# Computing the first norm in two token halves, with the token matrix loaded by halves around the first weights

## The chip, the cores and the metric

The kernel runs on one core of a Trainium2 chip. A core has five engines that each work through their own list of instructions in order: TensorE (PE in the profile, its weight loads PEld), VectorE (DVE), ScalarE (ACT), GpSimd (POOL) and SyncE (SP, which here does nothing but issue DMA transfers). Engines wait for each other through semaphores. The metric is the time of one execution on the device in microseconds (us); the median of three runs before the change is 925.3 us (924.67 to 925.98).

## The reference

One transformer layer for 128 context tokens and 512 latent tokens with 1024 features. The part that matters here is its beginning:

```python
def _rmsnorm(x, g):
    xf = x.astype(jnp.float32)
    inv = lax.rsqrt(jnp.mean(xf * xf, axis=-1, keepdims=True) + RMS_EPS)
    return (xf * inv).astype(x.dtype) * g
...
    sh1, sc1, g1, sh2, sc2, g2 = _modulation(c, w_mod, b_mod)   # silu(c) @ w_mod + b_mod
    h = _rmsnorm(x, n1) * (1 + sc1) + sh1
    aq, ak, av, bq, bk, bv, ga, gb = _mixer_inputs(h, w_in, qg, kg)   # h @ w_in, split
```

Context tokens and latent tokens have their own modulation vectors (`c_ctx` and `c`). Attention of two kinds, a merge, a second norm and an MLP follow; the change does not touch them.

## The kernel before

**Layout.** Features lie on the 128 partitions, tokens along the row: the token matrix is eight feature tiles of 128 x 640 (`NT = 640` columns, 128 context tokens and then 512 latent ones). `HALVES` are columns 0 to 319 and 320 to 639, which is as many as one matmul here writes (128x320). `SEGS[h]` cuts a half further where the two groups of tokens meet: half 0 is 128 + 192 columns, half 1 is 320, and `SEGS[2]` is the whole row as 128 + 512.

**Precision.** Operands of the large products are split in two, a high part (rounded to TensorE's short type, fp32r) and a low part (what is left). A product is three matmuls: high weights with high h, low weights with high h, high weights with low h.

**The stage in question** is the first 51 us. `squares` builds the mean of squares: ScalarE squares one feature tile, VectorE the next, VectorE adds them, and a matmul with a matrix of 1/1024 (`ones`, in full float32) sums over the partitions into `mean[h]`, once per half. `rstd_rows(h)` turns that into the reciprocal root with two ScalarE instructions (logarithm, exponential). For each feature tile f, `mod_product(f, q)` multiplies the conditioning vector with a 512 KB block of modulation weights (four matmuls for each of two blocks q), `mod_rows` copies the result out of PSUM, `mod_cols` (two matmuls) turns rows into columns, and two small VectorE instructions make scale and shift. `h_scaled` (VectorE) multiplies x by scale and reciprocal root into `xm`, `h_hi` (ScalarE) adds the shift and rounds (h0h, h1h, ... in the profile), `h_lo` (VectorE) makes the low part (h0l, ...).

`first_gemm(f, i, part)` multiplies feature tile f with three tiles of the input projection (i = 0, 1, 2) while the later modulations are computed; `w0_conv(q)` splits their weights for two feature tiles at a time, the high part on ScalarE, the low part on VectorE. One feature tile is 18 matmuls: for each of three weight tiles and each of two halves, three products. `warm(n)` issues n matmuls of `ones` by `ones` whose result nobody reads, from the table `WARM`; they are called fillers below.

**Order.** All this stands under `tc.manual_schedule`: each engine executes its instructions in the order in which the code writes them. SyncE issues loads in the order of the calls `x_load`, `mod_load`, `w0_load`; each transfer reuses one of eight semaphores, so a transfer is issued only when the one eight places ahead has landed.

Of the kernel before, what the change touches and what calls it, by code (L numbers as in the profile page):

```python
# [10 lines left out]
F32 = mybir.dt.float32  # L11
F32R = mybir.dt.float32r
AF = mybir.ActivationFunctionType
# [3 lines left out]
P = 128  # L17
NT = 640
HT = 320
KT = 8  # L20
# [25 lines left out]
OU = 1800  # L46
MG = 2
W2P = 2
WARM = (15, 3, 2, 5, 0, 0, 3)
NMS = 9  # L50
W0P = 0
WAH = (4, 6)
# [17 lines left out]
HALVES = (slice(0, HT), slice(HT, NT))  # L70
# [3 lines left out]
def trunk_layer(ctx: ExitStack, tc: tile.TileContext, xT, small_in, wmodA, wmodB, tabs, cacheK, cacheV, bias,  # L74
                w_in, w_br, w_out, w1, w2, yT, akT, avT, bkT, bvT):
    nc = tc.nc
    PE, ACT, DVE = nc.tensor, nc.scalar, nc.vector
# [29 lines left out]
    def u(name, dt=F32):  # L107
        return cur["p"].tile([P, NT], dt, tag="u", bufs=cur["nu"], name=name)
# [39 lines left out]
    p0 = open_phase("p0", 9)  # L148
# [8 lines left out]
    ones = cst.tile([P, P], F32, name="ones")  # L157
# [8 lines left out]
    def mod_load(f, qs=range(2)):  # L166
        for q in qs:
            st = p0.tile([P, 1024], F32, tag="ms", bufs=NMS, name="ms")
            nc.sync.dma_start(st, wmodA[f, :, q * 1024:(q + 1) * 1024])
            MS[f, q] = st  # L170

    def w0_load(q):
        for n in FIRST:
            W0S[n, q] = p0.tile([P, 256], F32, tag="ws", bufs=6, name="ws")
            nc.sync.dma_start(W0S[n, q], w_in[n][:, q * 256:(q + 1) * 256])

    xs = []

    def x_load(i):
        x = p0.tile([P, 2, NT], F32, tag="x2", bufs=4, name=f"x{i}")  # L180
        nc.sync.dma_start(x, xT[:, 2 * i:2 * i + 2, :])
        xs.extend(x[:, j] for j in range(2))
# [168 lines left out]
    b0 = [f() for f in (ps_s, ps_s, ps_s, ps_t, ps_g, ps_g)]  # L351
    acc0 = [(b0[2 * i][:, :HT], b0[2 * i + 1][:, :HT]) for i in range(3)]
    H1, rows, ss, xm, rstd = [], {}, {}, {}, u("rstd")

    def warm(n):

        for _ in range(n):
            PE.matmul(acc0[2][1][:, :P], ones, ones, start=True, stop=True)

    def mod_product(f, q):  # L360

        for k in range(4):
            g = 32 * k
            PE.matmul(pm[f % 2][g:g + 2, :256], sc_e[:, 4 * q + k], MS[f, q][:, k * 256:(k + 1) * 256],
                      start=q == 0, stop=q == 1, tile_position=(0, g))

    def mod_rows(f, eng=ACT):
        rows[f] = p0.tile([P, 256], F32, tag="mrow", bufs=2, name="mrow")
        if eng is DVE:
            for sl in (slice(P, 2 * P), slice(0, P)):  # L370
                DVE.tensor_copy(rows[f][:, sl], pm[f % 2][:, sl])
        else:
            ACT.activation(rows[f], pm[f % 2][:, :256], AF.Copy)

    def mod_cols(f):
        p = pm[f % 2]
        for i in (1, 0):
            PE.matmul(p[:, 256 + 2 * i:258 + 2 * i], rows[f][:, i * P:(i + 1) * P], sel, start=True, stop=True)
# [5 lines left out]
    SEG0 = SEGS[0] + SEGS[1]  # L384

    def h_scaled(f):
        xm[f] = u("xm")
        for sl, g in SEGS[2] if f else SEG0:
            DVE.scalar_tensor_tensor(xm[f][:, sl], xs[f][:, sl], ss[f][1][:, g:g + 1], rstd[:, sl],
                                     op0=OP.mult, op1=OP.mult)  # L390

    def h_hi(f, segs=None):
        if len(H1) == f:
            H1.append(h_pair(f"h{f}"))
        for sl, g in segs or SEGS[2]:
            ACT.activation(H1[f][0][:, sl], xm[f][:, sl], AF.Identity, bias=ss[f][0][:, g:g + 1])

    def h_lo(f):
        for sl, g in SEGS[2]:
            DVE.scalar_tensor_tensor(H1[f][1][:, sl], xm[f][:, sl], ss[f][0][:, g:g + 1], r32(H1[f][0][:, sl]),  # L400
                                     op0=OP.add, op1=OP.subtract)

    def first_gemm(f, i, part, hs=(0, 1)):

        ws = W0[i] if part == 0 else W0[i][:1]
        for w, h in [(w, h) for h in hs for w in ws] if f == 0 else [(w, h) for w in ws for h in hs]:
            PE.matmul(acc0[i][h], w[:, f], H1[f][part][:, HALVES[h]], start=f == 0 and w is W0[i][0] and part == 0,
                      stop=f == KT - 1 and part == 1)

    def w0_conv(q, tiles=range(3), parts="hl"):  # L410
        for i in tiles:
            ks = slice(2 * q, 2 * q + 2)
            st = W0S[FIRST[i], q].rearrange("p (k n) -> p k n", k=2)
            if "h" in parts:
                ACT.activation(W0[i][0][:, ks], st, AF.Copy)
            if "l" in parts:
                (DVE, nc.gpsimd)[W0P].tensor_sub(W0[i][1][:, ks], st, r32(W0[i][0][:, ks]))

    def squares(i, between=None):

        q, q2 = u("sq"), u("sq")
        ACT.activation(q, xs[2 * i], AF.Square)
        DVE.tensor_mul(q2, xs[2 * i + 1], xs[2 * i + 1])
        for sl in HALVES if i == 3 else (slice(0, NT),):
            DVE.tensor_add(q[:, sl], q[:, sl], q2[:, sl])
        for h in range(2):
            PE.matmul(mean[h][:, :HT], ones, q[:, HALVES[h]], start=i == 0, stop=i == 3)
            if between and h == 0:
                between()
# [14 lines left out]
    with tc.manual_schedule(engines={e.engine for e in (PE, ACT, DVE, nc.gpsimd, nc.sync)}):  # L444
        for f in range(2, KT):
            mod_load(f)
            if f % 2 == 0:
                w0_load(f // 2)
        for p in pm:
            DVE.memset(p[:, :256], 0.0)  # L450
        ACT.activation(sc_e, cc, AF.Exp, scale=-1.0)
        DVE.tensor_scalar(sc_e, sc_e, 1.0, None, op0=OP.add)
        DVE.reciprocal(sc_e, sc_e)
        DVE.tensor_mul(sc_e, sc_e, cc)
        DVE.tensor_scalar(b1, bm, 1.0, None, op0=OP.add)
# [11 lines left out]
        warm(WARM[4])  # L467
        mod_cols(0)
        warm(WARM[5])
        h_scaled(0)  # L470
        h_hi(0, SEG0)
        mod_product(1, 0)
        warm(WARM[6])
        w0_conv(0, (2,), "h")
        w0_conv(0, (1, 2), "l")
        first_gemm(0, 0, 0, (0,))
        mod_product(1, 1)
        first_gemm(0, 0, 0, (1,))
        mod_rows(1)
        h_lo(0)  # L480
        first_gemm(0, 1, 0)
        mod_cols(1)
        h_scaled(1)
        first_gemm(0, 2, 0)
        h_hi(1)
        for i in range(3):
            first_gemm(0, i, 1)
        for q in range(2):
            mod_product(2, q)
        mod_rows(2)  # L490
        h_lo(1)
        w0_conv(1)
        for f in range(1, KT - 1):
            if f + 2 < KT:
                first_gemm(f, 0, 0)
            mod_cols(f + 1)
            h_scaled(f + 1)
            if f + 2 < KT:
                mod_product(f + 2, 0)
            else:  # L500
                first_gemm(f, 0, 0)
            first_gemm(f, 1, 0)
            if f + 2 < KT:
                mod_product(f + 2, 1)
            h_hi(f + 1)
            if f + 2 < KT:
                mod_rows(f + 2)
            first_gemm(f, 2, 0)
            for i in range(3):
                first_gemm(f, i, 1)  # L510
            h_lo(f + 1)
            if f % 2 == 0 and f < KT - 2:
# [644 lines left out]
    for n in range(KT):  # L1157
# [17 lines left out]
        for h in range(2):  # L1175
            sl = HALVES[h]
# [613 lines left out]
```

## Time and profile before

| | us |
|---|---|
| median of three runs | 925.3 |
| the profiled execution | 923.14 |
| its span in the profile | 921.4 |
| PE busy in the span | 903.8 (98%) |
| opening fillers on PE | 1.06 to 6.58 |
| first square sum on PE | 7.86 |
| first matmul with h (feature tile 0) | 18.34 |
| first matmul of feature tile 1 | 23.33 |
| first matmul of feature tile 2 | 27.89 |
| first matmul with the next weights (L315) | 51.53 |

The profile is of one execution. Lines are L numbers of the kernel; a row names engine, line, operation, output, inputs and shape. A full float32 matmul is recorded as two instructions, so that 30 recorded fillers are 15 in the program. After the change the same code has other line numbers: the matmuls of fillers, squares, modulation, columns and feature tiles are L358, L427, L364, L378 and L407 before, and L356, L426, L362, L376 and L405 after.

### The profile page before, as it was taken

Reading aid. Unit: us, or ns where it says so; the run is one execution under the profiler, and the core shown is the slowest. Engines: PE = TensorE matmul, PEld = TensorE weight load, DVE = VectorE, ACT = ScalarE, POOL = GpSimd, SP = SyncE. Lnnn points to the kernel's source line nnn. Section 1 sums busy time; section 2 is a strip of 40 time slices with the busy share of each in tenths; the row PEclk is TensorE's granted clock in tenths of the full one; section 3 lists DMA queues with packets and bytes.
Section 4 is the critical chain, followed back from the end, with each engine's and each line's share of the span. In section 5 each row is a group of like instructions: output and inputs, shape, how many; then the busy total and the mean of one; then the engine's idle time right before and its main releaser. Section 6 shows DMA issues by size and latency. Waiting matters only on the chain.

```text
span 921.4 us, 16641 instructions
## 1 busy us (share of the span) xinstructions
PE 903.8 (98%) x6136; PEld 872.6 (95%) x6136; DVE 712.9 (77%) x1503; ACT 564.4 (61%) x1175; POOL 194.6 (21%) x225
## 2 busy tenths in 40 slices
PE   8999999999999999999999999999999999999996
PEld 6799889989999999999999999999999999999995
DVE  6675887857766697586689996986798778975897
ACT  4566777757656765755324577536754576447775
POOL 0020200002211001211130010445234432364140
PEclk9999999999999999999999999999999999999998
DMA  9893310115636389899742362888678877888475
GB/s 344 307 247 97 89 46 26 62 57 153 163 109 149 115 242 308 208 248 261 247 144 92 104 194 92 138 193 190 168 138 188 179 173 158 167 179 189 96 123 152
DMA packets 54321, 150.56 MB, mean 163 GB/s; under 512 B 6688, under 2 KB 10416, under 8 KB 54240
## 3 DMA queue, kind: packets, MB, share of 16 engines
q1 hardware_dynamic: 31440, 99.74, 32.9%
q0 software_dynamic: 21648, 48.45, 29.8%
q10 hardware_dynamic: 1152, 1.31, 0.4%
q8 instruction: 48, 0.79, 0.3%
q14 instruction: 33, 0.27, 0.1%
HBM read 137.15 MB, written 4.60 MB: 154 GB/s over the span
## 4 chain that ended last, share of the span: by engine, by line
PE 83%; DVE 7%; ACT 4%; DMA 3%; issue 2%; POOL 0%; DVEq 0%; SPq 0%; ACTq 0%; POOLq 0%
PE b L1657 12%; PE b L1658 12%; PE b L1659 12%; PE pg L315 6%; PE pg L316 6%; PE pg L317 6%; PE pss L317 3%; PE pss L315 3%; PE pss L316 3%; DVE mt L1102 2%; DMA wmt<-wmodB 2%; PE pt L317 2%; PE pt L315 2%; PE pt L316 2%; PE pt L694 1%
## 5 line engine op out<-in xcount | busy, mean ns | idle before, releaser
L1394 ACT ACTIVATE wb<-wsb 128x512 fp32r<-128x512 f32 x140 | 87.2, 628 | 89.5 <-PE b L1659 61.0
L1657 PE MATMUL b<-op,wb 128*128 128x320 f32 x448 | 138.6, 309 | 0.2 <-DVE x L1510 0.2
L1658 PE MATMUL b<-op,wb 128*128 128x320 f32 x448 | 138.5, 309 | 0.0
L1659 PE MATMUL b<-op,wb 128*128 128x320 f32 x448 | 138.4, 309 | 0.0
L1399 DVE TENSOR_TENSOR wb<-wsb,wb 128x512 fp32r<-128x512 f32 x124 | 91.5, 742 | 26.4 <-ACT wb L1394 26.3
L1402 POOL DMA_DIRECT2D wsb<-w x84 | 73.6, 911 | 128.6 <-DVE wb L1399 102.7
L1102 DVE SCALAR_TENSOR_TENSOR mt<-wmt,cb 128x512 f32<-128x512 f32 x128 | 80.7, 687 | 6.2 <-DMA wmt<-wmodB 6.2
L267 ACT ACTIVATE wh<-wst 128x512 fp32r<-128x512 f32 (+1 forms) x84 | 61.0, 740 | 39.7 <-PE pg L316 15.0
L1657 PEld LDWEIGHTS b<-op,wb 128*128 128x128 f32 x448 | 84.1, 188 | 0.9 <-DVE x L1510 0.9
L1658 PEld LDWEIGHTS b<-op,wb 128*128 128x128 f32 x448 | 84.1, 188 | 0.2 <-DVE op L1467 0.2
L1659 PEld LDWEIGHTS b<-op,wb 128*128 128x128 f32 x448 | 84.1, 188 | 0.0
L1379 POOL DMA_DIRECT2D wsb<-w x28 | 25.6, 914 | 137.2 <-DVE wb L1399 48.0
L633 DVE TENSOR_TENSOR pl<-pt,ph 128x512 fp32r<-128x512 f32 (+1 forms) x72 | 44.9, 627 | 12.0 <-ACT ph L632 10.1
L276 DVE TENSOR_TENSOR wl<-wst,wh 128x512 fp32r<-128x512 f32 (+1 forms) x55 | 43.0, 793 | 10.8 <-ACT wh L267 8.8
L1510 DVE SCALAR_TENSOR_TENSOR x<-b,parts,x 128x128 f32<-128x128 f32 (+1 forms) x116 | 46.3, 429 | 2.8 <-PE b L1659 2.0
L632 ACT ACTIVATE ph<-pt 128x512 fp32r<-128x512 f32 (+1 forms) x72 | 39.2, 548 | 13.9 <-PE po L702 3.9
L1394 ACT ACTIVATE wb<-wst 128x512 fp32r<-128x512 f32 x56 | 34.8, 626 | 16.2 <-PE b L1659 8.9
L1659 PE MATMUL b<-t,wb 128*128 128x320 f32 x144 | 44.5, 309 | 0.0
L1658 PE MATMUL b<-t,wb 128*128 128x320 f32 x144 | 44.5, 309 | 0.0
L1657 PE MATMUL b<-t,wb 128*128 128x320 f32 x144 | 44.5, 309 | 0.0
L1467 DVE TENSOR_TENSOR op<-hid,op 128x1280 fp32r<-128x1280 f32 (+2 forms) x32 | 36.9, 1155 | 7.6 <-ACT op L1466 7.4
L1510 DVE SCALAR_TENSOR_TENSOR x<-tp,parts,x 128x320 f32<-128x320 f32 (+2 forms) x60 | 38.5, 670 | 1.0 <-ACT tp L1561 1.0
(886 smaller groups left out, 3006.7 us busy)
## 6 DMA issues: line engine op xcount, KB each, us to landing
wsb<-w POOLq DMA_DIRECT2D x112, 256.0 KB, 5.2
wst<-w SPq DMA_DIRECT2D x36, 512.0 KB, 4.0
wmt<-wmodB SPq DMA_DIRECT2D x32, 512.0 KB, 4.4
wst<-w_in SPq DMA_DIRECT2D x31, 512.0 KB, 4.4
wsb<-w SPq DMA_DIRECT2D x28, 512.0 KB, 4.3
ms<-wmodA SPq DMA_DIRECT2D x16, 512.0 KB, 7.7
wl<-w_in POOLq DMA_DIRECT2D x9, 512.0 KB, 8.4
wst<-w_br SPq DMA_DIRECT2D x8, 512.0 KB, 6.5
```

The costliest lines, as they stand in the source:

```text
L267: ACT.activation(hi[:, ks], st[:, ks], AF.Copy)
L315: PE.matmul(ps, wh[:, k], xh[:, sl], start=first, stop=False)
L316: PE.matmul(ps, wh[:, k], xl[:, sl], start=False, stop=False)
L317: PE.matmul(ps, wl[:, k], xh[:, sl], start=False, stop=last)
L1102: DVE.scalar_tensor_tensor(t, st[:, q * 512:(q + 1) * 512], 1.0, r32(cb[2 * q + i][:, :512]), op0=OP.mult, op1=OP.mult, accum_out=parts[:, ...
L1394: ACT.activation(w[:, 0:4], t, AF.Copy)
L1399: (nc.gpsimd if o in BLKPOOL[l - 1] else DVE).tensor_sub(w[:, 4:8], t, r32(w[:, 0:4]))
L1402: nc.gpsimd.dma_start(t, self.src(l, c, n, e)[:, 4 * half:4 * half + 4], accum_op=OP.add)
L1510: DVE.scalar_tensor_tensor(X1[i][:, sl], src[:, sl.start - off:sl.stop - off], g[:, j:j + 1], X1[i][:, sl], op0=OP.mult, op1=OP.add)
L1657: PE.matmul(b, w[:, k], xh, start=not whole and k == 0, stop=False, skip_group_check=True)
L1658: PE.matmul(b, w[:, k], xl, start=False, stop=False, skip_group_check=True)
L1659: PE.matmul(b, w[:, 4 + k], xh, start=False, stop=o not in ("A11", "S2", "S1") and k == 3, skip_group_check=True)
```

## The change

The token matrix is loaded by halves: four transfers for the first 320 columns of all tiles, then the two modulation blocks of tile 0 and the first weights, then four transfers for the other columns. `squares(i, h)` works on one half at a time. The order of the work is written anew: the first half goes through squares, reciprocal root, scaling and rounding; its high part is multiplied with the high weights of feature tile 0 while the second half is squared; the second half follows. For the last two pairs of tiles in the second half VectorE does not add the two squares, and PE sums both (`whole` false). `WARM` changes, and two accumulators change places in PSUM (`b0`). The loop over feature tiles is written anew too.

```diff
-WARM = (15, 3, 2, 5, 0, 0, 3)
+WARM = (15, 2, 4, 3, 13, 2, 2)
...
-    for i in range(3):
-        x_load(i)
-    mod_load(0, (0,))
-    x_load(3)
-    mod_load(0, (1,))
+    def x_load(h):
+        for i in range(4):
+            nc.sync.dma_start(x2[i][:, :, HALVES[h]], xT[:, 2 * i:2 * i + 2, HALVES[h]])
+
+    x_load(0)
+    mod_load(0)
     w0_load(0)
+    x_load(1)
     mod_load(1)
...
+    def squares(i, h, whole=True):
+
+        t = u("sq")
+        q, sl = [t[:, x] for x in HALVES], HALVES[h]
+        ACT.activation(q[0], xs[2 * i][:, sl], AF.Square)
+        DVE.tensor_mul(q[1], xs[2 * i + 1][:, sl], xs[2 * i + 1][:, sl])
+        if whole:
+            DVE.tensor_add(q[0], q[0], q[1])
+        for j in range(1 if whole else 2):
+            PE.matmul(mean[h][:, :HT], ones, q[j], start=i == 0, stop=i == 3 and (whole or j == 1))
...
         warm(WARM[0])
-        for i in range(3):
-            squares(i)
-            warm(WARM[i + 1])
+        for i in range(4):
+            squares(i, 0)
+            warm(WARM[1])
         mod_product(0, 0)
-        squares(3, lambda: mod_product(0, 1))
-        w0_conv(0, (0,))
+        warm(WARM[2])
+        mod_product(0, 1)
         rstd_rows(0)
         mod_rows(0, DVE)
+        w0_conv(0, (0,), "h")
+        warm(WARM[3])
+        mod_cols(0)
+        h_scaled(0, 0)
         w0_conv(0, (1,), "h")
+        warm(WARM[4])
+        h_hi(0, 0)
+        w0_conv(0, (2,), "h")
+        for i in range(3):
+            first_gemm(0, i, 0, (0,), "h")
+        for i in range(4):
+            squares(i, 1, i < 2)
+            warm(WARM[5])
+        w0_conv(0, parts="l")
         rstd_rows(1)
...
+        for i in range(3):
+            first_gemm(0, i, 0, (0,), "l")
+        h_lo(0, 0)
         mod_product(1, 0)
+        mod_product(1, 1)
+        mod_rows(1)
+        h_scaled(0, 1)
+        h_hi(0, 1)
+        for i in range(3):
+            first_gemm(0, i, 1, (0,))
         warm(WARM[6])
         first_gemm(0, 0, 0, (1,))
...
         for f in range(1, KT - 1):
-            if f + 2 < KT:
-                first_gemm(f, 0, 0)
-            mod_cols(f + 1)
...
+            first_gemm(f, 0, 0)
+            if f == 1:
+                mod_product(2, 0)
+                mod_product(2, 1)
+                mod_rows(2)
+                w0_conv(1, parts="h")
             else:
+                mod_cols(f + 1)
+                h_scaled(f + 1)
...
             for i in range(3):
                 first_gemm(f, i, 1)
+            if f < 3:
+                for q in range(2):
+                    mod_product(f + 2, q)
+                mod_rows(f + 2)
             h_lo(f + 1)
+            if f == 1:
+                w0_conv(1, parts="l")
```

How this moves PE's list. In the rows, `ones` with 128x128 is a filler, `sq` a square sum, `ms` a modulation block, `mrow` the columns step, `w_...` the split weights (even numbers high, odd numbers low), and x15 says how often a row stands in succession. PE before the first matmul with h, from behind the opening fillers, before:

```order
L427 MATMUL pss<-sq,ones 128x320 x2
L358 MATMUL pg<-ones 128x128 x5
L364 MATMUL po<-ms,sc_e 2x256 x4
L427 MATMUL pss<-sq,ones 128x320
L364 MATMUL po<-ms,sc_e 2x256 x4
L427 MATMUL pss<-sq,ones 128x320
L378 MATMUL po<-pk,mrow 128x2 x2
L364 MATMUL pt<-ms,sc_e 2x256 x4
L358 MATMUL pg<-ones 128x128 x3
L407 MATMUL pss<-h0h,w_114 128x320
```

and now:

```order
L362 MATMUL po<-ms,sc_e 2x256 x4
L356 MATMUL pg<-ones 128x128 x4
L362 MATMUL po<-ms,sc_e 2x256 x4
L356 MATMUL pg<-ones 128x128 x3
L376 MATMUL po<-pk,mrow 128x2 x2
L356 MATMUL pg<-ones 128x128 x13
L405 MATMUL pss<-h0h,w_118 128x320
L405 MATMUL pt<-h0h,w_120 128x320
L405 MATMUL pg<-h0h,w_122 128x320
```

Ahead of the first h there were 15 + 13 fillers and 8 square sums; now there are 15 + 28 fillers and 4 square sums. The rows that follow on PE now, where feature tile 0 had its 18 matmuls in a piece with the modulation blocks of tile 1 between them:

```order
L426 MATMUL pss<-sq,ones 128x320
L356 MATMUL pg<-ones 128x128 x2
L426 MATMUL pss<-sq,ones 128x320
L356 MATMUL pg<-ones 128x128 x2
L426 MATMUL pss<-sq,ones 128x320 x2
L356 MATMUL pg<-ones 128x128 x2
L426 MATMUL pss<-sq,ones 128x320 x2
L356 MATMUL pg<-ones 128x128 x2
L405 MATMUL pss<-h0h,w_119 128x320
L405 MATMUL pt<-h0h,w_121 128x320
L405 MATMUL pg<-h0h,w_123 128x320
L362 MATMUL pt<-ms,sc_e 2x256 x8
```

Six square sums and eight fillers stand between the first three matmuls of tile 0 and the next three; two more fillers come further down. On VectorE, at the same place in the program, now:

```order
L386 SCALAR_TENSOR_TENSOR xm<-x_82,sc_249,rstd 128x320
L378 TENSOR_SCALAR sc_337<-pt,b_112,pk 128x2
L379 TENSOR_SCALAR sh_336<-pt,pk 128x2
L386 SCALAR_TENSOR_TENSOR xm<-x_82,sc_337,rstd 128x128
L386 SCALAR_TENSOR_TENSOR xm<-x_82,sc_337,rstd 128x512
L397 SCALAR_TENSOR_TENSOR h0l<-xm,sh_248,h0h 128x320
```

The low part of tile 0 in its second half (last row) stands behind the scale, the shift and the scaling of tile 1; before, the low part of tile 0 stood ahead of them.

More of the change, by code (lines that the diff above doesn't have):

```diff
@@ L175, in w0_load @@
             nc.sync.dma_start(W0S[n, q], w_in[n][:, q * 256:(q + 1) * 256])
[L177 to L182, printed above, removed]
-    for i in range(3):
-        x_load(i)
-    mod_load(0, (0,))
-    x_load(3)
-    mod_load(0, (1,))
+    x2 = [p0.tile([P, 2, NT], F32, tag="x2", bufs=4, name=f"x{i}") for i in range(4)]
+    xs = [x[:, j] for x in x2 for j in range(2)]
+    def x_load(h):
[3 more added lines that the diff above has]
+    mod_load(0)
     w0_load(0)
+    x_load(1)
     mod_load(1)
@@ L417, in w0_conv @@
                 (DVE, nc.gpsimd)[W0P].tensor_sub(W0[i][1][:, ks], st, r32(W0[i][0][:, ks]))
[L419 to L429, printed above, removed]
+    def squares(i, h, whole=True):
[7 more added lines that the diff above has]
+            PE.matmul(mean[h][:, :HT], ones, q[j], start=i == 0, stop=i == 3 and (whole or j == 1))
     def rstd_rows(h):
```

70 lines of the change are left out of this document (30 added, 40 removed).

## The prediction

> **What bounds the kernel now.** I read the page first, then the engines' busy time by stretches of the first 50 us, what PE waited for there, and the chain of waits through them.
>
> ```profile
> span 921.4 us, 16641 instructions
> PE 903.8 (98%) x6136; PEld 872.6 (95%) x6136; DVE 712.9 (77%) x1503; ACT 564.4 (61%) x1175; POOL 194.6 (21%) x225
> ...
> 6.60:18.30 11.70, 10.24 (x70) 6.83 (x70) 8.42 (x18) 5.84 (x13) 0.00 (x0) 1.00 1.01 374
> 18.30:27.90 9.60, 9.56 (x85) 7.00 (x86) 7.18 (x19) 5.07 (x12) 0.00 (x0) 1.00 1.04 397
> 27.90:50.00 22.10, 22.10 (x185) 17.71 (x184) 14.08 (x38) 12.29 (x28) 1.55 (x2) 1.00 0.75 255
> ...
> PE pss L427 <- DVE sq L425: 1.3, 1, 1.3
> PE pss L407 <- ACT h0h L396: 0.2, 1, 0.2
> ```
>
> The columns of a stretch are its length, then busy us of PE, PEld, DVE, ACT and POOL, the granted clock, the DMA share and GB/s. The last two rows are all that PE waited for between 6.6 and 50 us: 1.3 us for the first squares and 0.2 us for h0h. The 11.70 us stretch ahead of the first matmul with h holds 10.24 us of PE, so 1.46 us of it were idle. PE takes its list in order, and a filler or a square sum takes its turn like any other matmul; so what the change puts on PE between 6.6 and 28 us comes out at the end, less at most those 1.46 us. DMA is as full there (1.01, 1.04), so I also look at whether a transfer comes too late. Behind 50 us the rows of all engines stand in the same order as before, apart from a swap of two PSUM names, so the first stage decides.
>
> **The unit prices.** From the chain of waits (start, length, what; two records make one full float32 matmul):
>
> ```profile
> 7.86 1.34 PE pss L427 x4
> ...
> 9.87 1.08 PE pss L427 x4
> ...
> 12.53 1.11 PE pg L358 x10
> 13.64 0.54 PE po L364 x8
> ...
> 16.20 0.50 PE po L378 x4
> ...
> 17.50 0.79 ACT h0h L396 x2
> 18.34 0.56 PE pss L407 x2
> ...
> 22.42 0.97 PE po L364 x16
> ...
> 24.18 0.34 PE po L378 x4
> ...
> 25.06 0.35 PE pss L407
> 25.55 0.15 PE pss L407
> ...
> 28.05 0.59 PE pss L407 x4
> ```
>
> A square sum (320 columns, full float32) is 1.08/2 = 0.54 us; a filler 1.11/5 = 0.222; a modulation block 0.54 alone and 0.97 for two in succession; the columns step 0.34; a matmul of a feature tile 0.59/4 = 0.146, and about 0.1 more for the first behind float32 work (0.35 against two of them).
>
> **Term A, work added to PE: +6.6 us.** Fillers behind the opening 15 go from 13 to 38 (8, 4, 3, 13, 8, 2): 25 x 0.222 = 5.55. Square sums go from 8 to 10, because the last two pairs of the second half are summed on PE: 2 x 0.54 = 1.08. The other eight only change place.
>
> **Term B, idle time filled: -1.5 us.** The 1.46 us above is the most that can be had. The start confirms it:
>
> ```profile
> 1.06 5.52 PE L358 MATMUL pg<-ones 128*128 128x128 f32 x30 [1.06 <-DVE ones L158]
> ...
> 6.04 0.83 DVE sq L423
> 6.97 0.84 DVE sq L425
> ```
>
> The opening fillers end at 6.58, and before the first tile lands at 6.04. A half tile has half the bytes, so it lands some 0.8 us earlier (the next tile follows 1.57 us later, squares at 7.61 against 6.04); its multiply and add are two 128x320 instructions of 0.49 (row below), and PE begins sums right behind the opening fillers at about 6.6 instead of 7.86.
>
> ```profile
> L425 DVE TENSOR_TENSOR sq<-sq 128x320 f32<-128x320 f32 x2 | 0.9, 489 | 0.1
> ...
> 7.61 0.74 ACT L422 ACTIVATE sq<-x 128x640 f32<-128x640 f32 x1 [0.83 <-DMA x<-xT]
> ```
>
> The pace from there is PE's: a sum and two fillers are 0.54 + 0.44 = 0.98 us. The transfers' rate depends on the size of a piece, since each 5120-byte row of x is now read in 1280-byte pieces. The nearest rows are the stretch in which the 1 KB pieces of the first weights land, and one of large pieces:
>
> ```profile
> DMA packets 358, 0.52 MB, mean 307 GB/s; under 512 B 41, under 2 KB 294, under 8 KB 358
> ...
> DMA packets 459, 1.97 MB, mean 393 GB/s; under 512 B 50, under 2 KB 50, under 8 KB 459
> ```
>
> A half tile (328 KB) takes 0.83 us at 393 and 1.07 at 307 GB/s; I take the second, the nearer size. Four then cost 0.4 us more than PE's pace, against the 0.5 us by which the first is early: nothing, and at worst 1 us for all eight halves. [...]
>
> So PE ends the four sums at 6.6 + 3.9 = 10.5, the modulation blocks with four fillers between at 12.5, columns at 13.2, and 13 fillers (2.9 us) at about 16.5. h0h of the first half would be there earlier: before, it takes from the columns at 16.20 to 17.50 + 0.79 = 18.29, 2.1 us, and 13.2 + 2.1 is 15.3, plus 0.4 for the third weight tile's conversion. The fillers end last. The first matmul with h comes at 16.5 instead of 18.34, 1.8 us earlier, but without the second half of the squares, whose 3.24 us and eight fillers of 1.78 are now behind it. When x's second half lands is read from SP: its transfer in the eighth place behind the second modulation block is issued when that block has landed.
>
> ```profile
> 13.93 1.51 SPq L175 DMA_DIRECT2D ws<-w_in  x3
> ```
>
> By 13.93 the small inputs, all of x and that block, 3.8 MB, have landed; the change puts only the first weights ahead of the rest of x, 0.39 MB or 1.3 us at 307 GB/s. So the last half tile lands at 15.2 to 16.2 us, and PE reaches its last sum past 20: the fillers there cover no wait.
>
> **Term C, fewer switches: -0.7 us.** Two blocks in succession take 0.97 against 2 x 0.54 plus the slow first matmul of 0.2 more: 0.3 us each for tiles 1, 3 and 4, less some 0.2 for feature tile 0, which now comes in pieces.
>
> **Term D, new waits of PE: +3.0 us.** The duration of each link is in the rows of feature tile 3 (before):
>
> ```profile
> 28.47 0.50 PE L378 MATMUL pt<-pk,mrow 128*128 128x2 f32 x4
> ...
> 29.41 1.00 DVE L389 SCALAR_TENSOR_TENSOR xm<-x,sc,rstd 128x128 f32<-128x128 f32 x2
> ...
> 30.45 0.72 ACT L396 ACTIVATE h3h<-xm,sh 128x512 fp32r<-128x512 f32 x1 [0.26 <-DVE xm L389]
> 31.21 0.75 DVE L400 SCALAR_TENSOR_TENSOR h3l<-xm,sh,h3h 128x512 fp32r<-128x512 f32 x1 [0.53 <-ACT h3h L396]
> 31.88 1.09 DVE L417 TENSOR_TENSOR w<-ws,w 128x256 fp32r<-128x256 f32 x3
> ...
> L389 DVE SCALAR_TENSOR_TENSOR xm<-x,sc,rstd 128x320 f32<-128x320 f32 x1 | 0.5, 547 | 0.0
> ```
>
> From the start of the columns step, scaling is done after 30.41 - 28.47 = 1.94 us, the high part after 31.17 - 28.47 = 2.70, the low part after 3.49, the first low weight tile after about 3.87.
>
> D1, feature tile 0, second half: its low part stands on VectorE behind the scaling of tile 1, so it is ready 1.94 + 0.55 (128x320) = 2.5 us after the columns of tile 1. PE has 0.36 of columns and four matmuls (0.67) to do until then: it waits 1.4 us. Queued behind are all matmuls of tile 1.
>
> D2, start of tile 2: its columns stand late, behind 12 matmuls and two modulation blocks of tile 1. PE then has six matmuls (1.0) and two blocks (1.06): 0.36 + 2.06 = 2.4 us against 2.70 for h2h: 0.3 us.
>
> D3: the low weights of the second pair are made on VectorE behind the low part of tile 2. PE needs the first 0.4 us after h2h, at 3.1 us, and has it at 3.87: 0.8 us. Before, these conversions stood ahead of tile 2's scaling.
>
> D4, feature tile 6: the columns of tile 7 stood ahead of its matmuls and now stand behind four of them (0.59 us).
>
> ```profile
> 45.81 0.50 PE L378 MATMUL pt<-pk,mrow 128*128 128x2 f32 x4
> ...
> 47.79 0.72 ACT L396 ACTIVATE h7h<-xm,sh 128x512 fp32r<-128x512 f32 x1 [0.26 <-DVE xm L389]
> 48.54 0.75 DVE L400 SCALAR_TENSOR_TENSOR h7l<-xm,sh,h7h 128x512 fp32r<-128x512 f32 x1 [0.53 <-ACT h7h L396]
> 48.89 0.75 PE L407 MATMUL pss<-h7h,w 128*128 128x320 f32 x4
> 49.48 0.45 PE L407 MATMUL pss<-h7l,w 128*128 128x320 f32 x2
> ```
>
> h7h, ready at 48.51, moves to 49.10, past 48.89 where PE wants it (0.25 us with the handing over), and h7l from 49.29 to 49.88, past 49.73 (0.2): 0.45 us. Each of D1 to D4 is nothing if the link is not last, and up to 0.3 us more.
>
> **The sum.** 6.6 - 1.5 - 0.7 + 1.4 + 0.3 + 0.8 + 0.45 = +7.4 us. The profiled execution took 923.14 us (span 921.4), 2.2 under the median of 925.3; I add to the median: 932.7 us.
>
> Does it reach the end? PE waits little later, and the longest links on the chain that are not its own are loads of modulation weights, as the chain and SP's waits show:
>
> ```profile
> 337.97 9.35 DMA wmt<-wmodB
> ...
> SPq L1098 <- DVE mt L1102: 63.0, 23, 6.4
> ```
>
> Those loads are issued when VectorE has used up the tiles before them, so they move with the delay.
>
> **The rivals.**
>
> *The earlier first half pays (faster).* If the sums of the second half wait for x, their fillers and sums are free and the 1.8 us at the first matmul with h are kept to the end: 923.5 us. It decides if the last half tile lands later than about 21 us. For it speaks that DMA is full; against it, the 15.2 to 16.2 us above. Such a late landing would also hold up the later modulation blocks. 0.04.
>
> *The delay is absorbed later (the same).* If the loads of modulation weights at 338 us run on their own time, PE finds them ready and 7.4 us shrink towards nothing: 925.5 us. For it speaks the 9.35 us link; against it, SP's waits. 0.05.
>
> *The work counts, the waits do not.* If VectorE is ahead of what D1 to D4 assume, A, B and C are left: +4.4, 929.7 us. 0.15.
>
> *Transfers are slower too.* With x in small pieces 1 us late, and D at its upper bounds (4 x 0.3): +7.4 + 1.0 + 1.2 = +9.6, 934.9 us. For it speaks the full DMA; against it, that PE, by the sum, comes to each block of modulation weights after it has landed. 0.13.
>
> *The clock.* The opening fillers run at 5.52/15 = 0.37 us each and later ones at 0.222, with the granted clock at 1.00 in the rows throughout, so PE doubles its pace after a few us of work. In the change PE works without a pause from 1.06 us, and so did it before but for 1.3 us, after which fillers still took 0.222: no gain from more of them. [...]
>
> **How the numbers follow.** Forecast 0.63, rivals 0.04, 0.05, 0.15, 0.13. The range reaches from under the third case to over the fourth, 929.0 to 935.5 us. A difference of 0.2% (1.9 us) is about what a measurement of this kernel can tell from none. Slower by more: 0.63 + 0.15 + 0.13 = 0.91; within: 0.05; faster: 0.04.
>
> **What would show it.** In the changed profile: first sum at about 6.6, the first matmul with h (L405) near 16.5, PE without a wait from there to about 24.9, a wait of 1.4 us before the low part of tile 0, feature tile 1 at about 28.2 (23.33 before), tile 2 near 34, a wait of 0.8 for a low weight tile there, and the first matmul with the next weights near 59 us instead of 51.53. Wrong would be: fillers whose place is a wait for DMA, or a tile 1 that starts before 26 us.

## The result: slower by 0.85%

| | before | after |
|---|---|---|
| median of six runs, us | 925.64 (923.41 to 926.05) | 932.54 (931.81 to 936.11) |
| ratio | 1 | 1.0085, 95% interval 1.0069 to 1.0100 |
| the profiled execution, us | 923.14 | 932.1 |
| its span, us | 921.4 | 930.3 |
| first matmul with h | 18.34 | 17.25 |
| first matmul of feature tile 1 | 23.33 | 28.72 |
| first matmul of feature tile 2 | 27.89 | 34.40 |
| first matmul with the next weights | 51.53 | 59.74 |

By the ratio the change costs 7.9 us (6.4 to 9.3). The forecast was 932.7 us. The last row of the table is called the landmark below: 8.21 us of the 8.9 us between the two spans are there before 60 us.

### The profile page after: what moved, and what is told of

It is laid out like the page before. It is cut to its first block, busy times and chain, and to the rows that moved or that the text cites. A ratio compares the mean times of both kernels' runs of the same rounds, so it can differ in the third digit from the quotient of the medians.

```text
span 930.3 us, 16760 instructions
## 1 busy us (share of the span) xinstructions
PE 911.4 (98%) x6190; PEld 879.8 (95%) x6190; DVE 712.3 (77%) x1509; ACT 565.2 (61%) x1179; POOL 195.1 (21%) x225
## 4 chain that ended last, share of the span: by engine, by line
PE 83%; DVE 8%; ACT 4%; DMA 2%; issue 2%; POOL 1%; SPq 0%; DVEq 0%; ACTq 0%; POOLq 0%
PE b L1677 10%; PE b L1678 10%; PE b L1676 10%; PE pg L313 7%; PE pg L314 7%; PE pg L315 7%; PE pss L315 3%; PE pss L313 3%; PE pss L314 3%; PE pt L315 2%; PE pt L314 2%; PE pt L313 2%; PE pg L356 2%; PE pt L713 2%; DMA wsb<-w 1%
```

## The profile after

The head of the page, and the engines' busy time in the stretches that the prediction used (length, then busy us of PE, PEld, DVE, ACT, POOL, granted clock, DMA share, GB/s):

```profile
span 930.3 us, 16760 instructions
PE 911.4 (98%) x6190; PEld 879.8 (95%) x6190; DVE 712.3 (77%) x1509; ACT 565.2 (61%) x1179; POOL 195.1 (21%) x225
...
6.60:18.30 11.70, 11.70 (x94) 9.81 (x94) 5.63 (x16) 5.30 (x13) 0.00 (x0) 1.00 1.03 372
18.30:27.90 9.60, 8.60 (x63) 6.63 (x61) 4.51 (x13) 2.44 (x6) 0.00 (x0) 1.00 1.04 395
27.90:50.00 22.10, 20.80 (x180) 15.43 (x180) 13.72 (x37) 10.60 (x26) 0.66 (x1) 1.00 0.62 222
```

PE is now busy in the whole first stretch (11.70 us; 10.24 before), and has pauses behind it: 1.00 and 1.30 us, where it had 0.04 and none. What PE waited for between 6.6 and 60 us (us in total, times, longest):

```profile
PE pss L405 <- DVE h0l L397: 1.3, 1, 1.3
PE pss L405 <- DVE w L415: 0.6, 1, 0.6
PE pss L405 <- ACT h2h L393: 0.3, 1, 0.3
PE po L437 <- DVE silu_c L436: 0.2, 1, 0.2
```

The first three are D1, D3 and D2 of the prediction. The wait for squares that stood here before is gone. The same in order of time, from PE's own list (start, length, what, idle time ahead of it and its releaser):

```profile
6.99 0.70 PE L426 MATMUL pss<-sq,ones 128*128 128x320 f32 x2
...
14.35 3.15 PE L356 MATMUL pg<-ones 128*128 128x128 f32 x26
...
17.25 0.39 PE L405 MATMUL pss<-h0h,w 128*128 128x320 f32 x1
...
28.18 0.56 PE L405 MATMUL pss<-h0l,w 128*128 128x320 f32 x2 [1.27 <-DVE h0l L397]
28.72 0.74 PE L405 MATMUL pss<-h1h,w 128*128 128x320 f32 x4
34.40 0.56 PE L405 MATMUL pss<-h2h,w 128*128 128x320 f32 x2 [0.29 <-ACT h2h L393]
35.52 0.56 PE L405 MATMUL pss<-h2h,w 128*128 128x320 f32 x2 [0.56 <-DVE w L415]
...
59.74 0.31 PE L313 MATMUL pg<-h0h,wh 128*128 128x320 f32 x1
```

The 13 fillers at 14.35 end right where the first matmul with h begins. That one comes 1.1 us earlier than before the change, but tile 1 begins 5.4 us later.

The accounting fits. But an accounting in which PE never waits says what PE did, not what would happen if a part of it were left out: behind a busy engine a second limit can stand unseen. So the experiments take the terms away one by one. In each the landmark is given beside the median, because it repeats more closely (59.74 and 59.61 us in two profiles of the changed kernel, 51.53 and 51.16 in two whose first stage is that of the kernel before; where the opening fillers made a difference, the text says so), while medians carry some 2 us of uncertainty from what comes behind.

## Experiment 1: all 38 fillers away

```diff
-WARM = (15, 2, 4, 3, 13, 2, 2)
+WARM = (15, 0, 0, 0, 0, 0, 0)
```

> The changed kernel without the 38 fillers behind the opening 15. Theory 1, PE's list: PE took every filler in its turn and waited for nothing else there, so each is worth its 0.222 us: 38 x 0.222 = 8.4 us less, 924.1 us. Rival, a second limit behind PE: in the changed kernel the last half tile of x lands at 16.58 us, its squares are ready on VectorE at 19.09, two sums (1.08), the reciprocal root (0.53 + 0.47), the scaling (0.55) and the high part (0.55) follow, so the second half of feature tile 0 can't start before about 22.5 us against 25.32 with fillers: 2.5 to 2.8 us less, about 929.8 us, with PE waiting for squares and for h0h in the fillers' place. Rival, the clock: if the fillers held PE's pace, the matmuls of the first 25 us run at half pace without them, and the time is at or over the changed kernel's 932.5 us.

Measured: 932.95 us (932.56 to 936.19), ratio to before 1.0107 (1.0086 to 1.0128); landmark 60.01 us. Nothing was gained. PE's waits up to 34 us and the granted clock by stretches (length, PE busy, clock, DMA share, GB/s):

```profile
PE pss L405 <- ACT h0h L393: 2.0, 2, 1.7
PE pss L405 <- DVE h0l L397: 1.3, 1, 1.3
PE pss L426 <- DVE sq L424: 1.1, 4, 0.4
PE po L376 <- DVE mrow L369: 0.6, 1, 0.6
```

```profile
10.00:14.00 4.00, 2.12 (x22) 1.00 1.05 363
14.00:18.00 4.00, 3.26 (x8) 0.60 1.05 404
18.00:24.00 6.00, 5.68 (x40) 0.98 1.04 397
24.00:26.00 2.00, 0.73 (x4) 0.77 1.00 395
26.00:30.00 4.00, 4.00 (x24) 0.50 1.05 396
30.00:32.00 2.00, 2.00 (x10) 0.53 0.99 387
```

Two things took the 8.4 us. First the second limit: PE waits for squares, modulation rows and h0h in the fillers' place. The second half of tile 0 starts at 22.78 us (this rival said 22.5), and tile 1 at 26.60 instead of 28.72, which is 2.1 us and not 8.4. Then the clock: it fell to half twice, each time at a pause of PE (1.7 us for h0h, 1.27 us for h0l). By the stretches it was low for 3.4 us the first time, (1 - 0.60) x 2 x 4.00 + (1 - 0.98) x 2 x 6.00, and for 6.8 us the second, (1 - 0.77) x 2 x 2.00 + (1 - 0.50) x 2 x 4.00 + (1 - 0.53) x 2 x 2.00, and from 25.6 to about 31.8 us PE ran at about half its pace:

```profile
25.63 0.90 PE L405 MATMUL pss<-h0l,w 128*128 128x320 f32 x2 [1.27 <-DVE h0l L397]
...
26.60 1.27 PE L405 MATMUL pss<-h1h,w 128*128 128x320 f32 x4
27.80 1.88 PE L362 MATMUL po<-ms,sc_e 128*2 128x256 f32 x16
...
33.32 1.04 PE L362 MATMUL pt<-ms,sc_e 128*2 128x256 f32 x16
```

Four matmuls of tile 1 take 1.27 us against 0.74 in the changed kernel, two modulation blocks 1.88 against 1.04 behind the fall. From tile 1 to tile 2 PE needed 8.06 us (5.68 with fillers), and the 2.1 us were gone. The rival on the clock, which the prediction had set aside, holds here. The executions without a profile agree. Their mean clock over the span tells of falls: in the profiles it is 0.997 or 0.998 where the clock falls only at the very end of the program (0.61 over the last 6.4 us of the kernel before, where PE has no work), and a further fall of 3.4 us, as the first one here, takes about 0.002 off (half of 3.4 us in 930). Every execution of this experiment has 0.990 to 0.994.

## Experiment 2: the last ten fillers away

```diff
-WARM = (15, 2, 4, 3, 13, 2, 2)
+WARM = (15, 2, 4, 3, 13, 0, 0)
```

> The changed kernel without the last 10 fillers (8 between the sums of the second half, 2 behind the low part of feature tile 0). Theory 1, PE's list: 10 x 0.222 = 2.2 us less, 930.3 us. Rival, a second limit: these ten stand behind the landing of x (16.58 us), where VectorE's squares are ready at 16.8 + 0.49, 18.28, 18.69 and 19.09 us; with the sums at 0.54 each PE would still be ahead of few of them, so 1.8 to 2.2 us, nearly the same. If the 28 that stay ahead of it are what is hidden, then leaving out all 38 gives little more than leaving out these ten.

Measured: 931.04 us (928.94 to 932.09), ratio 1.0078 (1.0060 to 1.0095); landmark 59.61 us. Tile 1 came 1.42 us earlier (27.30), then the clock fell again:

```profile
22.00:26.00 4.00, 2.94 (x29) 1.00 1.03 405
26.00:30.00 4.00, 3.49 (x23) 0.59 1.05 397
30.00:34.00 4.00, 4.00 (x38) 0.98 0.62 234
```

PE's waits here are the same 1.3 us for h0l as in the changed kernel, and 0.3 us for h0h a little ahead of it. With the one alone the clock held, in both profiles of the changed kernel; with the two it fell. The expectation had left the clock out, and in this profile both its figures (1.8 to 2.2 us) missed: 0.13 us remained. But not every execution fell: three of the six have a mean clock of 0.995 or 0.996 and took 931.91 to 932.09 us, the other three 0.997 or 0.998 and 928.94 to 930.16 us. Where the clock probably held, the ten fillers were thus worth about 1.7 us (6.2 us over the kernel before, by the medians, instead of 7.9), near the figure that was expected.

## Experiment 3: fillers in the pauses only

Fifteen fillers instead of 38: three ahead of the columns of tile 0, seven behind them, and five in the wait D1. The last write an unused part of another PSUM bank, since their usual one already holds sums there.

```diff
-WARM = (15, 2, 4, 3, 13, 2, 2)
+WARM = (15, 0, 0, 3, 7, 0, 0)
...
         h_hi(1)
+        warm(5, pm[0][:, HT:HT + P])
         for i in range(3):
             first_gemm(0, i, 1, (1,))
```

> The changed kernel with 15 fillers behind the opening ones instead of 38, put where the run without fillers showed PE pausing: 3 ahead of the columns of feature tile 0, 7 behind them, 5 ahead of the low part of feature tile 0 (these into unused columns of another PSUM bank). Theory 1, the pauses let the clock fall: with them filled the clock stays at 1.00 and the delay that the other 23 fillers cost is saved up to the second limit: the first matmul with the next weights near 57.0 us (59.74 with 38 fillers, 60.01 with none), 2.5 to 3 us less than the changed kernel. Rival, the number of fillers holds the clock: with 15 it falls as with none, 59.5 to 60 us. Rival, the price of a filler is its 0.222 us whatever stands behind: 23 x 0.222 = 5.1 us less, 54.6 us.

Measured: landmark 56.52 us, 3.1 us ahead of the unaltered changed kernel, which was measured beside it:

> The changed kernel unaltered, beside the next three on the same chip. All theories: 8 to 9 us over the kernel before, the first matmul with the next weights near 59.7 us, the granted clock at 1.00 up to there. In the run without fillers the clock halved in two places; if that can happen to any run whatever its pauses, some execution of this kernel would show it before 60 us too.

That one measured 932.6 us (930.82 to 934.85), ratio 1.0087 (1.0068 to 1.0107), landmark 59.61, and its clock was 1.00 up to there. With the 15 fillers the clock stayed at 1.00 too, up to 60 us:

```profile
14.00:18.00 4.00, 3.33 (x16) 1.00 1.05 403
18.00:24.00 6.00, 5.68 (x44) 1.00 1.04 396
24.00:30.00 6.00, 5.85 (x53) 1.00 1.04 398
30.00:36.00 6.00, 5.15 (x54) 1.00 0.79 254
```

So in these profiles it is where the fillers stand that held the clock, not how many there are, and 23 of the 38 are worth at most 3.1 us together, not their 5.1 us on the list. (The opening fillers took 5.18 us in this execution and 5.98 in the one beside it, and experiment 4 shows that such a lead reaches the first matmul with h in the changed kernel; so 2.3 to 3.1 us are due to the edit.) The rest went into new waits (PE between 6.6 and 60 us):

```profile
PE pss L426 <- DVE sq L424: 1.6, 5, 0.6
...
PE po L362 <- DMA ms<-wmodA: 0.4, 1, 0.4
```

The median was 932.21 us (929.06 to 935.39), ratio 1.0080 (1.0057 to 1.0103): the 3.1 us do not show in it. Experiment 7 takes that up.

## Experiment 4: the waits D1, D3 and D4 away

```diff
-        mod_cols(1)
-        h_scaled(1)
         h_lo(0, 1)
+        mod_cols(1)
+        h_scaled(1)
...
-                w0_conv(1, parts="h")
+                w0_conv(1)
...
-            if f == 1:
-                w0_conv(1, parts="l")
-            elif f % 2 == 0 and f < KT - 2:
+            if f % 2 == 0 and f < KT - 2:
```

and for feature tile 6 `first_gemm(f, 0, 0)` behind the columns of tile 7 instead of ahead of them.

> The changed kernel with the three waits D1, D3 and D4 taken away by order alone, all work kept: the low part of feature tile 0 goes ahead of the scaling of tile 1 on VectorE, both parts of the second pair's weights are made ahead of tile 2's scaling, and the columns of tile 7 go ahead of the matmuls of tile 6 again. Theory 1, the waits count in full: 1.27 + 0.56 + 0.45 (an estimate, as in the prediction) = 2.3 us less, 930.2 us. Rival, each wait only moves to the next link: without D1 PE comes 1.3 us sooner to the first matmul of tile 1, whose high part is then last (columns at 25.72, 2.7 us to the high part), so D1 gives nothing, and 1.0 us is left, 931.5 us.

Measured: landmark 57.60 us, 2.1 us earlier, of which 0.5 us were there at the first matmul with h already (16.76 for 17.25, the opening fillers ran faster), so 1.65 us by the edit; median 934.07 us (931.07 to 936.77), ratio 1.0114 (1.0094 to 1.0134), no better than the changed kernel. PE's two longest waits between 6.6 and 58 us:

```profile
PE pss L405 <- ACT h1h L393: 1.0, 1, 1.0
PE pss L405 <- ACT h2h L393: 0.3, 1, 0.3
```

The low part of tile 0 is now in time, and PE waits 1.0 us for h1h one step later, as the rival said of D1: from the first matmul with h to tile 1 it takes 11.15 us instead of 11.47. From tile 2 to the landmark it takes 23.94 instead of 25.34, so D3 and D4 gave 1.4 us, more than the 1.0 that both theories had for them. The theories counted idle time; from start to start, D3 and D4 had cost just these 1.4 us in the changed kernel (worked out under term D below). The sum lies between the rival's 1.0 and the first theory's 2.3, by the rival's mechanism. The profiled execution lost it again behind 60 us (experiment 7).

## Experiment 5: all that can be mended, mended

Experiments 3 and 4 together, and VectorE adds all the squares again (`squares(i, 1)` instead of `squares(i, 1, i < 2)`). What is left of the change is the order by halves and the loads by halves, with the rewritten loop over the tiles.

> The changed kernel with all that can be mended in it: the waits D1, D3 and D4 taken away by order, the two unsummed squares added on VectorE again, and the 15 fillers in the pauses. What is left of the change is the order by halves and the loading by halves. Theory 1, the prediction's terms are all there is: A falls to 0.4, B and C stay at -1.5 and -0.7, D2 at 0.3, so it is level with the kernel before or 1.4 us ahead, the first matmul with the next weights at 50 to 51.5 us. Rival, the order costs by itself: x's second half lands at 16.58 us behind the first weights, the second half of feature tile 0 starts at about 22.3 and tile 1 at about 25.5 to 26 instead of 23.33, so 2.5 to 4 us remain: 54 to 55.5 us, and the whole 2.5 to 4 us over the kernel before.

Measured: 928.53 us (925.35 to 931.16), ratio 1.0046 (1.0030 to 1.0062); landmark 54.52 us. It is 4.2 us over the kernel before by the ratio and 3.0 us at the landmark: the rival holds, the order costs by itself. The start of the second half's squares on VectorE (L422 multiplies, L424 adds), the last square on ScalarE and PE's list show where:

```profile
13.59 0.48 DVE L422 TENSOR_TENSOR sq<-x 128x320 f32<-128x320 f32 x1
...
15.90 0.47 ACT L421 ACTIVATE sq<-x 128x320 f32<-128x320 f32 x1 [0.35 <-DMA x<-xT]
...
16.40 0.81 PE L426 MATMUL pss<-sq,ones 128*128 128x320 f32 x2 [0.19 <-DVE sq L424]
...
17.85 0.49 DVE L424 TENSOR_TENSOR sq<-sq 128x320 f32<-128x320 f32 x1
...
18.39 0.81 PE L426 MATMUL pss<-sq,ones 128*128 128x320 f32 x2 [0.19 <-DVE sq L424]
...
21.73 0.56 PE L405 MATMUL pss<-h0h,w 128*128 128x320 f32 x2 [0.32 <-ACT h0h L393]
```

The second half's sums come one microsecond apart, at the pace of VectorE, which multiplies and adds each pair, and the last ends at 19.2. VectorE begins these squares only at 13.59 us, behind the scaling of the first half. The last tile of x is there at 15.90, two microseconds before the last pair is added, so what sets the pace here is VectorE's list and not the transfers. Root, scaling and rounding follow, and PE multiplies with the second half of tile 0 from 21.73. In the kernel before it does so from 19.37, 2.4 us sooner:

```profile
19.37 0.85 PE L407 MATMUL pss<-h0h,w 128*128 128x320 f32 x4
```

Tile 1 begins at 24.81 against 23.33. That difference is smaller because the two modulation blocks of tile 2 (1.0 us) now stand behind its first matmuls, where the kernel before has them ahead of tile 1; tile 2 begins at 30.58 against 27.89. Short waits for h2h and the silu rows (0.3 and 0.2 us) are in the 3.0 us too.

## Experiment 6: two pieces of it in the kernel before

*25 fillers more*, ahead of the second half of the first matmuls, and nothing else:

```diff
         mod_product(1, 1)
+        warm(25)
         first_gemm(0, 0, 0, (1,))
```

> The kernel before with 25 more fillers in one place, ahead of the second half of the first matmuls of feature tile 0 (at about 22 us). It does no more of the change. Theory 1, PE's list: 25 x 0.222 = 5.55 us more, about 931.0 us, and everything behind moves by as much. Rival, absorbed: PE has waits behind it that the delay fills or transfers set the later times: nothing more than 1 us.

Measured: 929.96 us (926.40 to 933.02), ratio 1.0065 (1.0042 to 1.0087), 6.0 us; landmark 57.38 us, 5.85 later (0.27 of it already there at the first matmul with h). PE is the bound there, and a filler cost its full 0.222 us (5.58 us over the 25); nothing behind took it back.

*x by half tiles*, four transfers more:

```diff
-        nc.sync.dma_start(x, xT[:, 2 * i:2 * i + 2, :])
+        for sl in HALVES:
+            nc.sync.dma_start(x[:, :, sl], xT[:, 2 * i:2 * i + 2, sl])
```

> The kernel before with nothing changed but the loads of x: each tile by two transfers of a half one behind the other, so 1280-byte pieces and four more transfers on the queue. Theory 1 (as in the prediction, both rates): a half tile takes 0.83 to 1.07 us, eight of them 0 to 1 us more than four whole ones, in part hidden: the first matmul with the next weights at 51.5 to 52.5 us, the time within 1 us of the kernel before. Rival, small pieces cost more than that (the pieces of 1 KB moved at 307 GB/s against 393): over 1 us, 52.5 to 53.5 us.

Measured: landmark 51.78 us (+0.25), median 926.65 us (923.91 to 931.75), ratio 1.0016 (1.0001 to 1.0032). That is inside the first theory's 0 to 1, and no more than what lies between two profiles of one first stage (51.53 and 51.16 us, experiment 7): a cost of the small pieces is not clear of the scatter at the landmark. By the ratio it is 1.5 us (0.1 to 3.0), so whether the time stays within 1 us is not settled, and five of the twelve executions have the mean clock of a fall.

*None of the 13 fillers* that the kernel before has behind the opening ones (`WARM = (15, 0, 0, 0, 0, 0, 0)`):

> The kernel before without its 13 fillers behind the opening 15. Theory 1, in the kernel before too they stand in waits and hold the clock: without them PE is idle for some 4.3 of the 11.7 us ahead of the first matmul with h (1.46 + 13 x 0.222), that matmul comes no sooner than 18.0 us, the clock falls to half in that stretch for some 3 us, and the first matmul with the next weights comes at 52 to 53.5 us instead of 51.53. Rival, they only cost: PE's list is shorter by 2.9 us and the first matmul with the next weights comes at 48.6 us. Rival, they neither cost nor protect: 51.5 us, clock at 1.00.

Measured: 925.49 us (922.60 to 928.45), ratio 0.9998 (0.9982 to 1.0014); landmark 52.13 us, 0.6 later. The first matmul with h came 0.9 us earlier (17.42), then the clock fell (0.94 in the stretch from 16 to 18 us, 0.50 from 18 to 20):

```profile
16.00:20.00 4.00, 3.20 (x22) 0.72 1.04 409
20.00:24.00 4.00, 4.00 (x35) 0.86 1.03 404
```

So in this profile the first theory holds in kind, and its size is at the lower end; at the end of the program there is no difference. Eight of the twelve executions have a mean clock of 0.997 or 0.998 and a median of 924.71 us, where those of the kernel before with that clock have 924.63: leaving the fillers out gained nothing even where the clock probably held.

## Experiment 7: a pause at 130 us

Experiments 3 and 4 gained at the landmark and lost it behind. Their spans were 930.8 and 931.8 us, so 874.3 and 874.2 us lie behind the landmark, where the kernel before had 869.9 (921.4 - 51.53) and the changed kernel 870.6. Over twelve profiles these are two groups: 868.5 to 870.6 us in seven, 874.2 to 874.6 in five (experiments 1 and 4, the 15 fillers of experiment 3, and of experiment 6 the one with half tiles and the one without fillers). In those five, and in no other, the clock fell at one more place, where PE pauses in every kernel. First the kernel before, then the one with half tiles, the same work:

```profile
129.00:132.00 3.00, 1.41 (x8) 1.00 0.00 0
132.00:135.50 3.50, 3.50 (x26) 1.00 0.44 150
135.50:139.00 3.50, 3.43 (x22) 1.00 0.00 0
```

```profile
130.00:133.00 3.00, 1.42 (x8) 1.00 0.00 0
133.00:136.50 3.50, 3.50 (x15) 0.51 0.46 150
136.50:140.00 3.50, 3.50 (x25) 1.00 0.00 0
```

The pause is equally long, and only in the second execution the clock falls. The half pace itself costs some 1.2 us there, an estimate from the rows: in the 7 us behind the pause PE has 40 matmuls (15 + 25) instead of 48 (26 + 22), and 8 x 0.146 is 1.2. Where the rest of the 4 us comes from is not traced.

The fall here lasts 3.4 us by its stretch, (1 - 0.51) x 2 x 3.50, as long as the first one of experiment 1. The pause (1.59 and 1.58 us of idle time in the rows above, two waits together) is there in eleven of the twelve profiles, and the twelfth is the one below; in five of the eleven the clock fell behind it, in the other six it stayed at 1.00. So one and the same pause is followed by a fall in some executions and not in others; what decides it is not shown.

Three fillers were put into this pause of the kernel before, ahead of the first half of the projection's tile n = 3, on an unused bank:

```diff
+            if (n, h) in ((3, 0),):
+                for _ in range(3):
+                    PE.matmul(psum["last"][:, 1, :P], ones, ones, start=True, stop=True)
             pg = ps_g()
```

> The kernel before with three fillers at about 131 us, ahead of a tile of products that waits 0.9 us for its bank (they write an unused bank), in the one place behind 50 us where the clock fell in four of the ten profiles so far, after pauses that leave PE busy 1.4 us of 3. Theory 1, that pause lets the clock fall in some executions, and those take some 4 us longer behind the first matmul with the next weights (865.8 to 866.3 us to the last matmul, against 860.3 to 862.5): with it shortened by 0.67 us the clock stays at 1.00 in the profile, and the median is 0 to 2 us under the kernel before. Rival, the fall has nothing to do with the pause: the median is the same, and a fall there remains as likely. Rival, the fillers cost their 0.67 us and more: 0.7 us slower.

Measured: 925.27 us (922.26 to 927.83), ratio 1.0001 (0.9984 to 1.0017). In the profile the fillers took the place of the first of the two waits, the second (0.88 us) stayed, and the clock held (with 869.3 us behind the landmark):

```profile
129.00:132.00 3.00, 2.22 (x14) 1.00 0.00 0
132.00:135.50 3.50, 3.35 (x23) 1.00 0.41 150
```

The mean clock over the span was 0.997 or 0.998 in all twelve timed executions; of the 22 of the kernel before beside it, eight had 0.996 or less (median 925.95 us, the other fourteen 924.63). So the fillers probably keep the clock up here, and a fall goes with 1.3 us, but the median is the same and the times scatter as widely as before. The fall at 130 us is therefore not what sets the median, and it explains at most a part of why the gains of experiments 3 and 4 don't show in theirs. All six executions of experiment 3 have 0.995 or 0.996 (two of the twelve of the changed kernel do), which at 1.3 us each is less than the gain at its landmark; and the two of experiment 4 with 0.997 or more took 931.07 and 934.13 us, on average no less than the changed kernel. Where the rest goes stays open.

No kernel of these runs beats the kernel before.

## Why the prediction was right, and where it was not

**The path.** PE's list bounds the first stage, and what is delayed there reaches the end: 8.21 us at the landmark, 8.9 in the span, 7.9 by the ratio, against 7.4. The 25 added fillers in the kernel before moved landmark and time alike (5.85 and 6.0 us). The rival that the delay is absorbed later has fallen, and so has "the earlier first half pays": the 1.1 us at the first matmul with h are spent 11 us later. "The work counts, the waits do not" has fallen with the waits below, 2.6 us of them. "Transfers are slower too" was partly there: the last half tile landed 0.4 us past its forecast, and half tiles alone moved the landmark by 0.25 us (experiment 6), not 1.

**The times on the way.** The first sum came at 6.99 (6.6 forecast), because the opening fillers took 6.10 us in this execution and not 5.52; the first matmul with h at 17.25 (16.5), tile 1 at 28.72 (28.2), tile 2 at 34.40 (34), the landmark at 59.74 (59). PE had no wait from 17.25 to 26.90, past tile 1's columns at 25.72 (24.9), as said. That the landmark is so near is in part luck: the first matmul with h was 0.75 us late, and the stretch from there to tile 2 took 0.35 us less than the forecast, in spite of a longer D1.

**Term D** was forecast at 3.0. D1 was 1.27 us (1.4), D2 0.29 (0.3), D3 0.56 (0.8). D4 is not among the waits, but PE's list has it:

```profile
56.23 0.46 PE L405 MATMUL pg<-h6l,w 128*128 128x320 f32 x2
56.78 0.85 PE L405 MATMUL pss<-h7h,w 128*128 128x320 f32 x4
57.57 0.57 PE L405 MATMUL pss<-h7l,w 128*128 128x320 f32 x2
```

At 0.146 us each, h7h could start at 56.52 and h7l at 57.36; with 0.26 and 0.21 us D4 is 0.47 (0.45). Together 2.6. A wait of 0.17 us for the silu rows was not forecast. Idle time is less than what a wait costs. The rows count it from the end of the matmul ahead, 0.31 us after its start, while a matmul that need not wait starts 0.147 us after the one ahead; and the first behind a wait takes 0.25 us until the next. From start to start D1 cost 1.53 us, D2 0.36, D3 0.83 and D4 0.57, together 3.3, and the silu rows 0.33. So the term was right within 0.3 us.

**Term C** was too large a gain. Two blocks in succession take 0.97 or 0.98 us on the chain of waits, as before. From tile 2 to the landmark PE needs 25.34 us against 23.64, 1.70 more. D3, D4 and silu, from start to start, are 1.73 of them, so no more than some hundredths are left there of the 0.3 us that the two blocks of tile 4, now in succession, were to bring.

**Term A, and with it B,** is right as an account and wrong as a price. PE did work through 25 more fillers and waited for nothing there, so 5.55 us stand on its list. But the step "so what the change puts on PE comes out at the end" takes each of them as the cause. Of the 8.2 us, 3.1 go when 23 fillers are taken out and the pauses stay filled (experiment 3; up to 0.8 of it is the pace of the opening fillers), another 2.0 when D1, D3, D4 and the two extra square sums go as well (experiment 5), and 3.0 stay with the order by halves. The prediction has no such term: it gave the order a gain (B and C, -2.2), because it looked for the landing of x's second half and found it early enough for PE, at 15.2 to 16.2 us (16.6 in the trace). It did not follow the chain of the second half on the other engines: its squares stand on VectorE behind the scaling of the first half, and with sums, root, scaling and high part they reach 21.7 us even when PE waits for them (experiment 5).

**The clock.** "No gain from more of them", said of the fillers, has fallen. It rested on one pause of 1.3 us without a fall. (The 1.00 that the rows give for the first 5 us was no support either: the trace's record of the clock begins at 5.1 us, where the fillers go from 0.43 to 0.22 us each.) In these profiles the clock fell where PE was idle for 1.86 of 3 us (experiment 1, 12 to 15 us), 1.27 of 2 (experiment 1, 24 to 26), 1.56 of 4 (experiment 2, 23 to 27), 1.04 of 4 (14 to 18, without the 13 fillers of the kernel before) and some 1.6 us in the pause at 130 us (five times); it held with 1.27 of 4 (both profiles of the changed kernel, around 27 us) and, six times, behind the same pause at 130 us. So the idle time alone does not tell which; what else counts is not shown. With its fillers the changed kernel keeps its clock in both profiles (1.00 up to 60 us); the wrong step cost the forecast nothing, since no filler was to be removed.

## What to carry to other kernels

A sum of what stands on a busy engine's list forecasts well what adding to it costs, but not what removing gives: look for the chain behind it, here from the second half's squares on VectorE to the first product with it, before a filler or a term is called the cause. Splitting a serial start into halves pays only if the second half's chain, on every engine, ends no later than before. Dead work belongs into the pauses: fifteen fillers in the right places held the clock as well as 38 in these profiles (1.00 up to 60 us), and none at all gained nothing.

## What was not expected of the hardware

- The granted clock of TensorE fell to half with PE idle for less time than the clock then stayed low: 1.04 to 1.86 us idle within stretches of 2 to 4 us, then 3.4 us at 0.50 (in the stretch of 3.50 us with a mean of 0.51, and in experiment 2: (1 - 0.59) x 2 x 4.00 + (1 - 0.98) x 2 x 4.00 = 3.4), once 6.8 (experiment 1).
- The same pause (PE busy 1.41 or 1.42 of 3.00 us) was followed by a fall in five profiles and not in six others; what decides it is not shown.
- A wait of PE costs more than the idle time in its row: 1.53 us for 1.27, 0.83 for 0.56.
- Pieces of 1280 bytes instead of 5120 moved the landmark by no more than 0.25 us over the 2.6 MB of x, though DMA is full in that stretch (a share of 1.01 from 6.6 to 18.3 us before); two profiles with the whole rows lie 0.37 us apart.
